# A two-layer diffusion backbone: the MLP output gates as rows from transposes in place of split diagonals, and the last row's sum of three squares on VectorE

## The chip, the cores and the metric

The kernel runs on one core of a Trainium2 chip. The metric is the device time of one execution in microseconds (us), of the whole program from its first to its last instruction. The kernel before takes 1154.96 us, the median of 3 runs (1154.93 to 1155.19). The profile is of one more execution, which took 1155.58 us.

## The reference, cut to what matters

512 latent tokens and 256 context tokens, each a row of 1024 numbers, go through two layers. A layer is a token mixer (pooling in layer 0, attention in layer 1) and an MLP with a squared ReLU and 4096 hidden units. The last layer drops the context.

```python
def rms_norm(x, g):
    return x * lax.rsqrt(jnp.mean(x * x, axis=-1, keepdims=True) + EPS) * g

for i in range(DEPTH):
    sh1, sc1, gt1, sh2, sc2, gt2 = ada_mods(c, w_ada[i], b_ada[i])        # rows of 1024 numbers; ctx has its own
    ...
    x = x + gt1 * rms_norm(y_lat, g_mix_post[i])
    m_lat = jnp.square(jax.nn.relu(modulate(rms_norm(x, g_mlp_pre[i]), sh2, sc2) @ w_mlp_in[i])) @ w_mlp_out[i]
    x = x + gt2 * rms_norm(m_lat, g_mlp_post[i])
```

The change concerns `gt2 * g_mlp_post`, the gate of the MLP's output (for the latent tokens of both layers and for the context tokens of layer 0), and the last `rms_norm`.

## The kernel before, in words

**Tiles and number formats.** Tokens lie in tiles t of 128 rows: 0 to 3 are latent, 4 and 5 context. A product of float32 matrices is three matmuls: each operand is split into a high half (a rounded copy, from ScalarE) and a low half (operand less high half, from VectorE), and high x high, high x low and low x high are added in PSUM. Weights come in pieces of 1 MB by DMA and are split on the way (the halves stand in `units`, L170 and L173). PSUM has two double banks (`psA`) and four single ones (`psB`); three work tiles of 128x1024 in SBUF (`tmp`, called `work`, `diag` or the like) go round.

**The gate.** The conditioning vector's product with `w_ada` ends as columns: entry n of gate k stands in partition n mod 128, column n div 128 (L315, `psada`, gathers the partial sums). The MLP's output has the 1024 channels along a row, so the gate must be turned, and be the same in each of the 128 partitions. The program has two ways. `gate_cols` (L322), in both, multiplies the columns by `g_mlp_post`, one short VectorE operation.
- `gate_diag` (L342 to L356): splits the 8 columns into high and low halves (L346, L347), multiplies the 128x128 identity by them, which gives two tiles `diag` of 128x1024 on VectorE (L350), sums each over the partitions by a matmul of 512 columns against ones (L355: two to a bank, four to a gate), and copies the two banks `psg` to `gate` on ScalarE (L356).
- `gate_rows` (L334) with `gate_half` (L326): transposes each column, broadcast over 128 columns, against the identity, which gives 128x128 of the row per transpose (L332: four to a bank, eight to a gate), and copies the banks to `gate` on ScalarE (L340). The mixers' gates `GT1` are made in this way.

`gate_diag` is called three times: twice in `before0` (L1272), between layer 0's MLP and what follows, for the latent tokens (ci 0) and the context (ci 1), and once in layer 1's last part (L1072), at the step time 5.1.

**The middle.** Layer 0's MLP runs over groups of 256 hidden units. A group is `Seven.run` (L770): seven chains of 12 matmuls, 384 tokens wide (L761, `psin`), into the double banks, with copies on ScalarE (L773 and its like) and two additions on VectorE (L777 and the next), and then `out_mm` (L884): the second product, 6 or 12 matmuls of 512 columns for each half of a row tile, into two banks `pso`, that `out_ev` adds to the sum in `acc` (L898 on VectorE). The last group goes through `finish` (L900) with `last0` (L1231) as its list of steps: for each row tile in turn the mean square (L201 on ScalarE), the power of -1/2 on GpSimd (`rstd`, L214 and L216), the gate (L362), the residual (L365), the next norm, and for each pair of tiles `norm_pair`: transposes (L386, `psx`), scale and shift (L394 on VectorE, the same on ScalarE for other columns), the high half (L400 or L408 on ScalarE) and the low half (L401 or L409 on VectorE), written to `ra`. From those the projections of attention start (L1141, `psq`).

**The end.** In layer 1's last part `finish` goes over the four latent tiles. The last tile's product stands in three banks, 512, 256 and 256 columns wide (`LAST`), and its squares, gates and residual work on these pieces straight from PSUM. `last_rstd` (L1189) adds the first two of the three sums of squares and EPS on GpSimd, the third on ScalarE (L1194), and takes the power on GpSimd (L1195). `norm_g` (L1197) multiplies the three pieces by the gate (L362, kept in program order); the residual (L365) and the store follow.

**The order.** In most places the order on an engine isn't that of the code: the framework's scheduler places instructions by a simulated timeline, and the code's own order (lists of steps with a due time each, `Steps`, L69) sets which comes first where two are ready. `keep_in_program_order` pins an instruction. So a step that is changed at one place can move others at another place.

Of the kernel before, what the change touches and what calls it, by code (L numbers as in the profile page):

```python
# [17 lines left out]
P = 128  # L18
# [76 lines left out]
def backbone(ctx: ExitStack, tc, x, ctx_in, w_ada, w_pool, w_qkv, g_q, g_k, w_o, w_mlp_in,  # L95
# [129 lines left out]
    onesr = const.tile([P, 2], F32R, name="onesr")  # L225
    ve.memset(nhalf, -0.5)
    ve.memset(cond, 0.0)
    ve.tensor_scalar(out=onesr, in0=ident[:, 0:2], scalar1=0.0, scalar2=1.0, op0=ALU.mult, op1=ALU.add)
# [112 lines left out]

    def gate_diag(i, m, ci, to=None):  # L342
        to = ci if to is None else to
        gc = gate_cols(i, m, ci)
        gh = small.tile([P, 2, KT], F32R, tag="gh", name="gh", bufs=2)
        ve.tensor_copy(gh[:, 0, :], gc)  # L346
        ve.tensor_tensor(out=gh[:, 1, :], in0=gc, in1=gh[:, 0, :], op=ALU.subtract)  # L347
        dg = [tmp.tile([P, KT, P], F32R, tag="t", name="diag") for _ in range(2)]
        for z, d in enumerate(dg):
            ve.tensor_tensor(out=d, in0=ident.unsqueeze(1).broadcast_to([P, KT, P]),  # L350
                             in1=gh[:, z, :].unsqueeze(2).broadcast_to([P, KT, P]), op=ALU.mult)
        for h in range(2):
            ps = psB.tile([P, 512], F32, tag="b", name="psg")
            for z, d in enumerate(dg):
                te.matmul(ps, onesr[:, 0:1].broadcast_to([P, P]), d[:, 4 * h:4 * h + 4, :], start=(z == 0), stop=(z == 1))  # L355
            sc.copy(gate[:, to, 512 * h:512 * h + 512], ps)  # L356
# [582 lines left out]
    def mlp1(inner, second, last):  # L939
# [132 lines left out]
        finish(1, [(NG - 2 + q, last_[q].hid, wo_[q]) for q in range(2)], range(NL), last, ((5.1, gate_diag, 1, GT2, 0),))  # L1072
# [108 lines left out]
    def norm_a(t, cols=HALVES):  # L1181
        ss = sm_tile("ss")
        if cols == LAST:
            return last_rstd(t, ss)
        for n, (c0, w) in enumerate(cols):
            mean_square(accv[:, t, c0:c0 + w], ss[:, n:n + 1])
        rs[t] = rstd(ss, len(cols))

    def last_rstd(t, ss):  # L1189
# [4 lines left out]
        sc.activation(ms[:, 1:2], ss[:, 2:3], AF.Identity, scale=1.0, bias=ms[:, 0:1])  # L1194
        gp.tensor_tensor(out=rs[t][:, 0:1], in0=ms[:, 1:2], in1=nhalf[:, 0:1], op=ALU.pow)  # L1195
# [410 lines left out]
```

## Time and profile before

| | |
|---|---|
| median of 3 runs | 1154.96 us |
| the profiled execution | 1155.58 us |
| its span, from the first instruction shown to the last | 1153.7 us |
| TensorE's granted clock, mean | 0.999 of full speed |
| matmul instructions / VectorE / ScalarE / GpSimd | 6200 / 1517 / 1082 / 113 |
| idle time of VectorE in front of L898, waiting for TensorE's L884 | 39.4 us |
| HBM read and written | 138.96 MB and 7.34 MB, 127 GB/s over the span |

How to read the rows shown further down. A row of the timeline has the start (us from the span's start), the time to the end of the last of its instructions, the engine, the line, the operation, its result and operands by the program's names, its shape and type, and the count of like instructions in a row; in brackets the time that the engine stood idle before it, and what ended that. PE is TensorE, PEld its load of weights, DVE VectorE, ACT ScalarE, POOL GpSimd. Matmuls are pipelined: one starts before the one ahead has ended, so the time that a matmul takes from the others is the distance between starts. A row of a table by windows has the stretch, its length, and for TensorE, its weight loads, VectorE, ScalarE and GpSimd the busy time and the count, then the granted clock, the share of the DMA engines and their GB/s. A row of one operation's instances has its durations in ns (shortest, middle, longest) and where the first and the last of them stand.

### The profile page before, as it was taken

What the parts mean: (1) busy time and instruction counts of PE and PEld (TensorE: products, weight loads), DVE (VectorE), ACT (ScalarE), POOL (GpSimd) and SP (SyncE); (2) the same over time, 40 slices, a digit from 0 to 9 for tenths busy, and PEclk for the clock granted to TensorE, in tenths of its full rate; (3) what the DMA queues carried; (4) which work ended last, traced back from release to release, by engine and by line L of the source; (5) the groups of instructions that cost most, each with busy time, mean ns of one, the idle gap of its engine ahead of it and who ended that gap; (6) DMA issues with size and microseconds to landing.
All of it is one profiled execution on the core that took longest, in us unless ns stands there. A gap on an engine that the chain in (4) does not pass through costs nothing.

```text
span 1153.7 us, 16000 instructions
## 1 busy us (share of the span) xinstructions
PE 1135.3 (98%) x6200; PEld 988.7 (86%) x6200; DVE 930.9 (81%) x1517; ACT 632.1 (55%) x1082; POOL 71.1 (6%) x113
## 2 busy tenths in 40 slices
PE   7999999999999999999999999999999999999997
PEld 6779899988899988998887889988988888888886
DVE  4788588998988997996778699867787679778876
ACT  7687445554455444455675367753776435534523
POOL 1230000000000000000241200002100000000001
PEclk9999999999999999999999999999999999999999
DMA  9982233333343444333422102115243214313312
GB/s 376 419 350 75 74 116 113 137 120 141 113 150 140 146 147 146 120 137 115 177 74 73 37 1 74 38 74 186 106 159 133 91 56 146 110 45 138 110 33 114
DMA packets 25516, 147.34 MB, mean 128 GB/s; under 512 B 2784, under 2 KB 5344, under 8 KB 9696
## 3 DMA queue, kind: packets, MB, share of 16 engines
q1 hardware_dynamic: 25440, 146.32, 35.0%
q8 instruction: 49, 0.80, 0.3%
q14 instruction: 27, 0.22, 0.1%
HBM read 138.96 MB, written 7.34 MB: 127 GB/s over the span
## 4 chain that ended last, share of the span: by engine, by line
PE 90%; issue 3%; POOL 3%; DVE 2%; ACT 2%; DMA 0%; POOLq 0%; DVEq 0%; SPq 0%; ACTq 0%
PE pso L884 24%; PE psin L761 18%; PE psin L637 16%; PE pso L995 12%; PE psy L1421 3%; PE po L1396 3%; PE pss L1355 3%; PE psq L1141 2%; PE pspt L1377 2%; PE psin L91 2%; PE psada L91 1%; POOL rs L216 1%; PE psm L91 1%; PE pspool L91 1%; POOL rs L1150 1%
## 5 line engine op out<-in xcount | busy, mean ns | idle before, releaser
L884 PE MATMUL pso<-units,rb 128*128 128x512 f32 x1152 | 279.2, 392 | 0.0
L884 PEld LDWEIGHTS pso<-units,rb 128*128 128x128 f32 x1152 | 214.7, 188 | 41.0
L303 DVE SCALAR_TENSOR_TENSOR rows<-raw,cond,rows 128x256 f32<-128x256 f32 x280 | 127.0, 478 | 2.0
L898 DVE TENSOR_TENSOR acc<-acc,pso 128x512 f32<-128x512 f32 x126 | 83.9, 679 | 39.5 <-PE pso L884 39.4
L637 PE MATMUL psin<-ra,rb 128*128 128x512 f32 (+1 forms) x310 | 87.8, 360 | 0.0
L995 PE MATMUL pso<-units,pairs 128*128 128x512 f32 x336 | 82.7, 389 | 0.0
L637 PE MATMUL psin<-ra 128*128 128x512 f32 (+1 forms) x256 | 76.5, 376 | 0.0
L995 PEld LDWEIGHTS pso<-units,pairs 128*128 128x128 f32 x336 | 63.1, 188 | 13.1
L999 DVE TENSOR_TENSOR acc<-acc,pso 128x512 f32<-128x512 f32 x72 | 48.7, 682 | 26.3 <-PE pso L995 26.3
L214 POOL TENSOR_SCALAR ms<-ss 128x1 f32<-128x1 f32 x15 | 10.0, 666 | 938.2 <-ACT junk L201 917.0
L761 PE MATMUL psin<-ra,units 128*128 128x384 f32 x336 | 65.8, 337 | 0.4 <-ACT psin L773 0.4
L761 PE MATMUL psin<-sums,units 128*128 128x384 f32 x336 | 64.1, 337 | 0.0
L761 PEld LDWEIGHTS psin<-ra,units 128*128 128x128 f32 x336 | 59.9, 188 | 4.0 <-ACT psin L773 0.5
L637 PEld LDWEIGHTS psin<-ra,rb 128*128 128x128 f32 x310 | 55.6, 189 | 8.7
L761 PEld LDWEIGHTS psin<-sums,units 128*128 128x128 f32 x336 | 59.0, 188 | 1.6
L173 DVE TENSOR_TENSOR units<-raw,units 128x1024 fp32r<-128x1024 f32 (+2 forms) x49 | 55.1, 1150 | 6.3 <-ACT units L170 6.1
L170 ACT CAST units<-raw 128x1024 fp32r<-128x1024 f32 (+2 forms) x49 | 47.0, 995 | 17.6 <-PE pso L884 13.4
L637 PE MATMUL psin<-rb 128*128 128x512 f32 (+1 forms) x155 | 55.9, 362 | 0.6 <-DVE rb L1490 0.6
L637 PEld LDWEIGHTS psin<-ra 128*128 128x128 f32 x256 | 47.1, 188 | 8.7
L896 ACT COPY acc<-pso 128x512 f32<-128x512 f32 x48 | 27.1, 586 | 47.3 <-PE pso L884 46.6
L1141 PE MATMUL psq<-units,ra 128*128 128x512 f32 x216 | 52.2, 393 | 0.0
L637 PE MATMUL psin<-rb,ra 128*128 128x512 f32 (+1 forms) x128 | 48.1, 376 | 0.0
(291 smaller groups left out, 2386.5 us busy)
## 6 DMA issues: line engine op xcount, KB each, us to landing
raw<-in_w_ada SPq DMA_DIRECT2D x48, 1024.0 KB, 6.2
raw<-in_w_mlp_in SPq DMA_DIRECT2D x32, 1024.0 KB, 4.9
raw<-in_w_mlp_out SPq DMA_DIRECT2D x32, 1024.0 KB, 5.3
raw<-in_w_qkv SPq DMA_DIRECT2D x6, 1024.0 KB, 4.9
spill<-xr SPq DMA_DIRECT2D x10, 512.0 KB, 3.8
xr<-spill SPq DMA_DIRECT2D x10, 512.0 KB, 6.5
raw<-in_w_o SPq DMA_DIRECT2D x4, 1024.0 KB, 4.9
xr<-in_x SPq DMA_DIRECT2D x4, 512.0 KB, 5.2
```

Source lines behind the costliest of these rows:

```text
L91: return lambda *args, **kw: self.tc.keep_in_program_order(f(*args, **kw))
L170: a = sc.copy(hi, raw)
L173: b = ve.tensor_tensor(out=lo, in0=raw, in1=hi, op=ALU.subtract)
L303: ve.scalar_tensor_tensor(out=r, in0=raw[:, k, :], scalar=cond[:, k, c:c + 1], in1=r, op0=ALU.mult, op1=ALU.add)
L637: te.matmul(ps[:, bank, o:o + ln], w[:, k, fs], rhs, start=start, stop=(k == KT - 1 and n == 2), skip_group_check=len(ks) < KT or self.paired)
L761: te.matmul(bank, w[k], a[k], start=start and k == 0 and m == 0, stop=stop and k == 3 and m == 2, skip_group_check=True)
L884: te.matmul(pss[h][:, 0:cols[h][1]], a[:, f, ts_], w[:, f, cols[h][0]:sum(cols[h])], start=(n == 0 and not seeded[t]), stop=(n == len(seq) ...
L898: ve.tensor_tensor(out=d, in0=d, in1=ps[:, 0:w], op=ALU.add)
L995: te.matmul(ps, a, w, start=(m == 0), stop=(m == len(seq) - 1))
L999: ve.tensor_tensor(out=M[n][:, t], in0=M[n][:, t], in1=ps, op=ALU.add)
L1141: te.matmul(ps, a[:, k, sl], w[:, k % 4, :], start=(k == 0 and n == 0), stop=(k == KT - 1 and n == 2))
L1355: te.matmul(ps[:, c2, 0:384], a[:, sl], b[:, kv, 384 * c2:384 * c2 + 384], start=(n == 0), stop=(n == 2))
```

## The change

1. `gate_diag` goes, with its constant `onesr` and the operation that makes it; its three calls become calls of `gate_rows` at the same places.
2. The last row's sum of the three squares: the third is added on VectorE in place of ScalarE, by an instruction that stands between the second and the third gated piece and is kept there; the power on GpSimd follows it. The scalar operations before (the squares, the first addition on GpSimd) are as before.

```diff
-    onesr = const.tile([P, 2], F32R, name="onesr")
...
-    ve.tensor_scalar(out=onesr, in0=ident[:, 0:2], scalar1=0.0, scalar2=1.0, op0=ALU.mult, op1=ALU.add)
...
-    def gate_diag(i, m, ci, to=None):
-        to = ci if to is None else to
-        gc = gate_cols(i, m, ci)
-        gh = small.tile([P, 2, KT], F32R, tag="gh", name="gh", bufs=2)
-        ve.tensor_copy(gh[:, 0, :], gc)
-        ve.tensor_tensor(out=gh[:, 1, :], in0=gc, in1=gh[:, 0, :], op=ALU.subtract)
-        dg = [tmp.tile([P, KT, P], F32R, tag="t", name="diag") for _ in range(2)]
-        for z, d in enumerate(dg):
-            ve.tensor_tensor(out=d, in0=ident.unsqueeze(1).broadcast_to([P, KT, P]),
-                             in1=gh[:, z, :].unsqueeze(2).broadcast_to([P, KT, P]), op=ALU.mult)
-        for h in range(2):
-            ps = psB.tile([P, 512], F32, tag="b", name="psg")
-            for z, d in enumerate(dg):
-                te.matmul(ps, onesr[:, 0:1].broadcast_to([P, P]), d[:, 4 * h:4 * h + 4, :], start=(z == 0), stop=(z == 1))
-            sc.copy(gate[:, to, 512 * h:512 * h + 512], ps)
...
-        finish(1, [(NG - 2 + q, last_[q].hid, wo_[q]) for q in range(2)], range(NL), last, ((5.1, gate_diag, 1, GT2, 0),))
+        finish(1, [(NG - 2 + q, last_[q].hid, wo_[q]) for q in range(2)], range(NL), last, ((5.1, gate_rows, 1, GT2, 0),))
...
     def norm_a(t, cols=HALVES):
         ss = sm_tile("ss")
         if cols == LAST:
-            return last_rstd(t, ss)
+            final.append(last_rstd(t, ss))
+            return
...
-        sc.activation(ms[:, 1:2], ss[:, 2:3], AF.Identity, scale=1.0, bias=ms[:, 0:1])
-        gp.tensor_tensor(out=rs[t][:, 0:1], in0=ms[:, 1:2], in1=nhalf[:, 0:1], op=ALU.pow)
+        return ss, ms, rs[t]
+
+    def last_pow(ss, ms, r):
+        tc.keep_in_program_order(
+            ve.tensor_scalar(out=ms[:, 1:2], in0=ss[:, 2:3], scalar1=ms[:, 0:1], scalar2=None, op0=ALU.add))
+        gp.tensor_tensor(out=r[:, 0:1], in0=ms[:, 1:2], in1=nhalf[:, 0:1], op=ALU.pow)
...
         for n, (c0, w) in enumerate(cols):
+            if cols == LAST and n == len(cols) - 1:
+                last_pow(*final[0])
             z = gated(t, yg[t], pso[t][n][:, 0:w] if cols == LAST else accv[:, t, c0:c0 + w], c0, c0 + w, pool)
...
-        gate_diag(0, GT2, 0)
-        gate_diag(0, GT2, 1)
+        gate_rows(0, GT2, 0)
+        gate_rows(0, GT2, 1)
```

In the code of the change the functions behind L340 have numbers that are lower by 18, and in `norm_a` and behind it by up to 9: its L743 is L761 of before, L866 is L884, L880 is L898, L344 is L362, L347 is L365, L376 is L394, L383 is L401.

What moves on the engines. **TensorE between the layers**, behind the last small gathering of conditioning sums (`psada`): the last group's chains (`psin`), the gates (`psg`), and its second products (`pso`). Two chains of 12 (L761, with `ra`, `units` and then `rb`, `ra`) stand ahead of the first row here. Before:

```order
L355 MATMUL psg<-diag,onesr 128x512 x2
L761 MATMUL psin<-sums,ra 128x384
L761 MATMUL psin<-rb,ra 128x384
L761 MATMUL psin<-sums,ra 128x384 x2
L761 MATMUL psin<-rb,ra 128x384
L761 MATMUL psin<-sums,ra 128x384 x7
L355 MATMUL psg<-diag,onesr 128x512 x2
L761 MATMUL psin<-ra 128x384 x12
L355 MATMUL psg<-diag,onesr 128x512 x2
L884 MATMUL pso<-units,rb 128x512 x12
L355 MATMUL psg<-diag,onesr 128x512 x2
L884 MATMUL pso<-units,rb 128x512 x84
```

The same place of the change, from `psada` and with those two chains:

```order
L313 MATMUL psada<-parts,sel 32x8 x4
L330 MATMUL psg<-ident,gc 128x128 x16
L743 MATMUL psin<-ra,units 128x384 x12
L743 MATMUL psin<-rb,ra 128x384 x12
L743 MATMUL psin<-sums,ra 128x384
L743 MATMUL psin<-rb,ra 128x384
L743 MATMUL psin<-sums,ra 128x384 x2
L743 MATMUL psin<-rb,ra 128x384
L743 MATMUL psin<-sums,ra 128x384 x7
L743 MATMUL psin<-ra 128x384 x12
L866 MATMUL pso<-units,rb 128x512 x96
```

The four pairs of matmuls, which stood apart between the chains and the second products, have become 16 transposes in a row ahead of the last group's chains, which are alike in both. Further on, between the 16 transposes `psx` of one pair of tiles and the 14 of the next that feed L408, stand 56 other matmuls where there were 72; the 14 that feed L394 at 577.60 us of the profile before have 24 ahead of them since the last two `psx`, where there were 19. The columns of layer 0's gates, of which these transposes are made, stand in VectorE's order some 300 rows ahead of the place that the splits for the diagonals had.

**VectorE a little later**, where the tiles 4 and 5 are scaled and shifted (L394, L376 in the change) and split into low halves (L401, L383). Before:

```order
L394 TENSOR_SCALAR acc<-psx,avec_95,mods_92 128x256 x3
L898 TENSOR_TENSOR acc<-acc,pso 128x512
L394 TENSOR_SCALAR acc<-psx,avec_95,mods_92 128x256 x3
L898 TENSOR_TENSOR acc<-acc,pso 128x512
L362 TENSOR_TENSOR work<-acc,gate 128x512
L401 TENSOR_TENSOR ra<-acc,ra 128x2x256
L173 TENSOR_TENSOR units<-raw,units 128x512
L362 TENSOR_TENSOR work<-acc,gate 128x512
L173 TENSOR_TENSOR units<-raw,units 128x512
L401 TENSOR_TENSOR ra<-acc,ra 128x2x256
```

The same place of the change:

```order
L880 TENSOR_TENSOR acc<-acc,pso 128x512 x2
L344 TENSOR_TENSOR work<-acc,gate 128x512
L376 TENSOR_SCALAR acc<-psx,avec_95,mods_92 128x256 x3
L344 TENSOR_TENSOR work<-acc,gate 128x512
L376 TENSOR_SCALAR acc<-psx,avec_95,mods_92 128x256 x3
L173 TENSOR_TENSOR units<-raw,units 128x512 x2
L347 SCALAR_TENSOR_TENSOR xr<-work,rs,xr 128x1024
L880 TENSOR_TENSOR acc<-acc,pso 128x512
L383 TENSOR_TENSOR ra<-acc,ra 128x2x256
L880 TENSOR_TENSOR acc<-acc,pso 128x512
L173 TENSOR_TENSOR units<-raw,units 128x512 x2
L383 TENSOR_TENSOR ra<-acc,ra 128x2x256
```

Between the last L394 and the first low half stood an addition and a gate before; in the change two halves of a weight, a residual and an addition stand there.

**VectorE's last instructions**, the last tile's gated pieces and residuals. Before:

```order
L365 SCALAR_TENSOR_TENSOR xr<-work,rs,xr 128x512 x2
L362 TENSOR_TENSOR work<-pso,gate 128x512
L362 TENSOR_TENSOR work<-pso,gate 128x256 x2
L365 SCALAR_TENSOR_TENSOR xr<-work,rs,xr 128x640
L365 SCALAR_TENSOR_TENSOR xr<-work,rs,xr 128x384
```

The same place of the change:

```order
L347 SCALAR_TENSOR_TENSOR xr<-work,rs,xr 128x512 x2
L344 TENSOR_TENSOR work<-pso,gate 128x512
L344 TENSOR_TENSOR work<-pso,gate 128x256
L1183 TENSOR_SCALAR ms<-ss,ms 128x1
L344 TENSOR_TENSOR work<-pso,gate 128x256
L347 SCALAR_TENSOR_TENSOR xr<-work,rs,xr 128x640
L347 SCALAR_TENSOR_TENSOR xr<-work,rs,xr 128x384
```

The sum (L1183) has come between the second and the third piece. In layer 0's MLP, from 290 to 492 us of the profile before, and up to the end of the projections for keys and values, near 620 us, TensorE, VectorE and ScalarE have the same instructions in another order; ahead of it and from there on to layer 1's last part, the rows are alike but for the numbers of buffers. GpSimd's rows are alike everywhere. On SP's queue the second of the three last loads of projection weights (L151) stands ahead of three of the four loads of the rotary tables (L1120), behind which it stood before.

More of the change, by code (lines that the diff above doesn't have):

```diff
@@ L1187, in norm_a @@
         rs[t] = rstd(ss, len(cols))
+    final = []
     def last_rstd(t, ss):
@@ L1470, in attention @@
         at(45.691, lambda: split(*raws[3], q=3))
-        at(39.281, gate_diag if False else gate_rows, 1, GT1, 0)
+        at(39.281, gate_rows, 1, GT1, 0)
     def output(st, base):
```

## The prediction

> **What bounds the kernel now.** I read the page first (the span, the busy shares, the chain that ended last), then the timeline of the three places that the change touches.
>
> ```profile
> span 1153.7 us, 16000 instructions
> PE 1135.3 (98%) x6200; PEld 988.7 (86%) x6200; DVE 930.9 (81%) x1517; ACT 632.1 (55%) x1082; POOL 71.1 (6%) x113
> PE 90%; issue 3%; POOL 3%; DVE 2%; ACT 2%; DMA 0%; POOLq 0%; DVEq 0%; SPq 0%; ACTq 0%
> ```
>
> TensorE holds 90% of the chain, so an edit pays only where it takes TensorE time away, ends one of the few waits of TensorE, or shortens the end after its last matmul. VectorE is busy 81% of the span, yet work taken from it is worth nothing by itself: the six diagonals and their splits are VectorE time beside a running TensorE. What a matmul costs is the distance of starts, not the duration, since matmuls overlap.
>
> **Place 1, the last gate (1126 to 1131 us).**
>
> ```profile
> 1129.90 1.09 PE L355 MATMUL psg<-diag,onesr 128*128 128x512 f32 x4
> 1130.82 1.52 PE L884 MATMUL pso<-ra,units 128*128 128x512 f32 x6
> 1132.18 1.52 PE L884 MATMUL pso<-units 128*128 128x512 f32 x6
> ```
>
> Six 512-wide matmuls take 1132.18 - 1130.82 = 1.36 us, 0.227 each. The four diagonal matmuls take 1130.82 - 1129.90 = 0.92. TensorE shows no idle time here, so this is on the path. Eight transposes replace them, and transposes of the same kind (fp32, 128 columns, against the identity) stand in the trace:
>
> ```profile
> 577.60 1.69 PE L386 MATMUL psx<-ident,acc 128*128 128x128 f32 x14
> 579.05 6.83 PE L884 MATMUL pso<-units,rb 128*128 128x512 f32 x29
> 585.72 1.91 PE L386 MATMUL psx<-ident,acc 128*128 128x128 f32 x16
> ```
>
> From 577.60 to 585.72 are 8.12 us; 29 matmuls take 29 x 0.227 = 6.58, so 14 transposes cost 1.54, or 0.11 each. Eight cost 0.88: **-0.04 us**. On VectorE the gate's columns alone are left, without the splits and diagonals behind them, so the transposes are not late.
>
> **Place 2, the two gates between the layers (536 to 554 us).**
>
> ```profile
> 540.43 2.35 PE L761 MATMUL psin<-ra,units 128*128 128x384 f32 x12 [0.43 <-ACT psin L773]
> 544.71 0.62 PE L355 MATMUL psg<-diag,onesr 128*128 128x512 f32 x2
> 546.05 1.39 PE L761 MATMUL psin<-sums,ra 128*128 128x384 f32 x7
> 547.47 0.73 PE L355 MATMUL psg<-diag,onesr 128*128 128x512 f32 x2
> 547.47 0.56 DVE L777 TENSOR_TENSOR work<-work,psin 128x384 f32<-128x384 f32 x1
> 548.08 2.36 PE L761 MATMUL psin<-ra 128*128 128x384 f32 x12
> 550.28 0.62 PE L355 MATMUL psg<-diag,onesr 128*128 128x512 f32 x2
> 550.74 2.89 PE L884 MATMUL pso<-units,rb 128*128 128x512 f32 x12
> 553.47 0.62 PE L355 MATMUL psg<-diag,onesr 128*128 128x512 f32 x2
> 553.93 6.33 PE L884 MATMUL pso<-units,rb 128*128 128x512 f32 x27
> ```
>
> Three of the four pairs of diagonal matmuls cost TensorE time: 550.74 - 550.28 = 0.46, 553.93 - 553.47 = 0.46, and as much the one at 544.71, together 1.38 us. The fourth, at 547.47, costs nothing: the chain before it ends at 546.05 + 1.39 = 547.44, L777 must read that bank before the next chain may write it (547.47 + 0.56 = 548.03), and the next chain starts at 548.08. That wait stays when the pair goes, and no other work stands in it. So of four pairs one is no gain.
>
> The 16 transposes now stand together, between the small psada matmuls and the chain at 540.43. They cost 16 x 0.11 = 1.76 us and fill the 0.43 us in which TensorE waits for L773: 1.33 more. A matmul starts before the one ahead ends (the pair at 550.28 takes 0.62 and is passed after 0.46), so they can begin 0.16 earlier: 1.17. The place gives 1.17 - 1.38 = **-0.2 us** (0 at the other end). Their inputs, the gate's columns, stand some 300 rows ahead in VectorE's order. Of the four ScalarE copies of the gates two stood beside the chains; now all four do, ahead of a relu that waits for L777 anyway.
>
> **Place 3, what is reordered (290 to 492 and 554 to 620 us).** The scheduler places the same instructions otherwise.
>
> ```profile
> 290.00:492.00 202.00, 202.00 (x1023) 181.82 (x1022) 179.10 (x340) 96.14 (x144) 0.00 (x0) 1.00 0.40 141
> ```
>
> In the first stretch TensorE is busy all 202 us, and two independent streams (the next group's psin, this group's pso) lie before it: I take 0, with +0.6 us as the far end (a wait as long as the longest below) and nothing to win. In the second, the kernel before has two waits that may go:
>
> ```profile
> 611.78 0.30 PEld L1141 LDWEIGHTS psq<-rb,ra 128*128 128x128 f32 x2 [0.34 <-ACT ra L408]
> 613.09 2.14 PEld L1141 LDWEIGHTS psq<-rb,ra 128*128 128x128 f32 x10 [0.59 <-DVE ra L409]
> ```
>
> They are 0.93 us. In the order of the change, 56 matmuls in place of 72 stand between the two groups of transposes there, so those that feed L408 come 16 x 0.227 = 3.6 us earlier; VectorE's table work keeps its place among what it waits for. On the other side the first low half for the projections comes later: VectorE does two weight halves (L173) and a residual (L365) ahead of it, where before they stood behind:
>
> ```profile
> 579.40 1.45 DVE L394 TENSOR_SCALAR acc<-psx,avec,mods 128x256 f32<-128x256 f32 x3 [0.55 <-PE psx L386]
> 583.92 0.69 DVE L401 TENSOR_TENSOR ra<-acc,ra 128x512 fp32r<-128x512 f32 x1
> 587.38 4.81 PE L1141 MATMUL psq<-rb,ra 128*128 128x512 f32 x20
> 589.34 1.28 DVE L173 TENSOR_TENSOR units<-raw,units 128x512 fp32r<-128x512 f32 x2
> 591.45 1.27 DVE L365 SCALAR_TENSOR_TENSOR xr<-work,rs,xr 128x1024 f32<-128x1024 f32 x1
> ```
>
> Before, the low half begins 583.92 - 579.40 = 4.5 us after the first L394, and 3.5 us ahead of its projections. The added 1.28 + 1.27 us take it to 586.5, and the L394 themselves come 0.8 later (in the order 24 matmuls in place of 19 stand ahead of their transposes: 5 x 0.227 = 1.1, less the 0.2 above): 587.3. TensorE starts six matmuls on high halves at about 587.2, so it asks for the low half at 588.5: 1.2 us to spare if nothing waits. On SP's queue a weight load now stands ahead of three of the four loads of the rotary tables:
>
> ```profile
> 590.64 27.90 SPq L151 DMA_DIRECT2D raw<-in_w_qkv  x2
> 605.59 0.69 DVE L1126 TENSOR_TENSOR acc<-acc,grow 128x512 f32<-128x512 f32 x1
> ```
>
> It goes out at 590.64, when the last L173 has freed its buffer; the tables are first touched at 605.59, 15 us later, so their loads cost nothing. For the stretch I take **-0.1 us**, between +1.1 and -0.93.
>
> **Place 4, the end.**
>
> ```profile
> 1148.09 0.42 DVE L362 TENSOR_TENSOR work<-pso,gate 128x256 f32<-128x256 f32 x1 [0.94 <-ACT junk L201]
> 1148.53 0.56 POOL L1195 TENSOR_TENSOR rs<-ms,nhalf 128x1 f32<-128x1 f32 x1 [1.54 <-ACT ms L1194]
> 1149.12 1.42 DVE L365 SCALAR_TENSOR_TENSOR xr<-work,rs,xr 128x640 f32<-128x640 f32 x2 [0.61 <-POOL rs L1195]
> ```
>
> L1194 goes; the same sum stands on VectorE ahead of the third gated piece. Its like is at the program's start:
>
> ```profile
> 6.01 0.15 DVE L91 TENSOR_SCALAR ms<-ss 128x1 f32<-128x1 f32 x1 [4.25 <-ACT junk L91]
> 6.25 0.56 POOL L492 TENSOR_TENSOR rs<-ms,nhalf 128x1 f32<-128x1 f32 x1 [4.96 <-DVE ms L91]
> 6.84 0.75 DVE L91 TENSOR_SCALAR acc<-xr,rs 128x1024 f32<-128x1024 f32 x1 [0.68 <-POOL rs L492]
> ```
>
> The power starts 0.24 after the sum's start, and the operation that uses it 0.59 after that. The third gated piece waited for the last square (its bracket), which the sum needs too, so the sum starts at 1148.09, the power at 1148.33 and the residual at 1148.92 in place of 1149.12: **-0.20 us**. Queued behind the sum is that piece; its 0.42 us lie under the power, to about 1148.66. If it held the power back until then, the residual would start at 1148.66 + 0.59 = 1149.25, +0.13 us. Rows of both kinds:
>
> ```profile
> 587.67 1.31 POOL L214 TENSOR_SCALAR ms<-ss 128x1 f32<-128x1 f32 x1 [6.61 <-DVE acc L898]
> 588.74 0.68 DVE L898 TENSOR_TENSOR acc<-acc,pso 128x512 f32<-128x512 f32 x1
> 589.07 0.56 POOL L216 TENSOR_TENSOR rs<-ms,nhalf 128x1 f32<-128x1 f32 x1
> 591.68 2.06 POOL L216 TENSOR_TENSOR rs<-ms,nhalf 128x1 f32<-128x1 f32 x1
> ```
>
> The power at 589.07 took 0.56 beside an L898, which reads one operand from PSUM as the gated piece does; the one at 591.68 took 2.06 beside L365, with both from SBUF. I take no hold. The Trainium skill (SBUF — State Buffer, section "SBUF: two separate sides") says that VectorE with two SBUF inputs locks a port pair that GpSimd's reads share; by it the gated piece, with one PSUM input, doesn't hold the power: the two rows agree.
>
> **Sum.** -0.04 - 0.2 - 0.1 - 0.20 = -0.54 us. The profiled execution took 1155.58 us, 1.88 more than its span, so its like would take 1155.04. It is 0.62 above the median of the runs, 1154.96; the difference carries over: **1154.4 us**. What a measurement of this kernel can tell from no change is about 0.2%, 2.3 us, so the forecast is within it.
>
> **Rivals.**
> 1. Slower: TensorE waits for the low halves at about 588 us. The L365 that now stands ahead of them waits for a sum and a power on GpSimd that come while L173 runs, with both its inputs in SBUF. Held ones took 1.31 and 2.06 us above, 3.4 together, where a free power takes 0.56 and a free sum less: some 2.4 longer. 1.2 us of it is to spare, so it costs 2.4 - 1.2 = 1.2, and the total is -0.44 + 1.2 = +0.8: 1155.7 us. It decides from 1.2 us of hold on, and turns the sign at 1.65. For it: those rows are of this very stretch. Against: before, the same holds were absorbed.
> 2. The two waits at 611 to 613 go and nothing new comes: -0.44 - 0.93 = -1.4, 1153.6 us. Against: L408 is reached through VectorE, which has no less to do.
> 3. Transposes don't overlap.
>
> ```profile
> L332 PE MATMUL psg<-ident,gc x8: 271/272/273, 764.9 to 766.7; 128*128 128x128 f32 x8
> ```
>
> At 0.272 each, Place 2 gives 16 x 0.272 - 0.43 - 1.38 = +2.54 and Place 1 8 x 0.272 - 0.92 = +1.26; with the end, +3.6: 1158.6 us. The 14 at 577.60 speak against it. The Trainium skill (TensorE: Matmul & The Clock Gate, "Part 4: PE-mode transpose") gives about 275 ns for a 128x128 transpose within a kernel: that is the duration here, and the 0.11 us between starts differ from it, so the measurement decides.
> 4. The stretch from 290 to 492 us gets waits of its own, one to four of 0.6 us: -0.54 + 0.6 to + 2.4, 1155.0 to 1156.8 us.
>
> That the change doesn't do what it says is excluded by the order: the sum stands between the second and third piece, and no diagonal is left.
>
> **Chances.** Forecast (1153.9 to 1155.0) 0.5; rival 1 0.25; rival 2 0.15; rival 3 0.03; rival 4 0.07. The range for eight in ten reaches over rivals 1 and 2 with the bounds of the reordered stretches: 1153.0 to 1156.4 us. Faster by over 0.2% needs rival 2 and more, 0.08; slower by over 0.2% is rival 3 and the far ends of 1 and 4, 0.10; within, 0.82.
>
> **What would show it.** The profile after should have 16 transposes right behind psada near 540 us, still a wait of TensorE for L777 near 548, the chain into the last layer 0.2 us earlier; no wait for low halves near 588 (else rival 1), less than 0.9 us of waits near 612; eight transposes of 0.88 us near 1130; and a power of 0.56 us that starts 0.24 after the sum, with the residual 0.83 after the sum's start. A held power, a TensorE wait in the two reordered stretches, or a distance of transposes over 0.11 us would make the forecast wrong.

## The result: 1.2% slower, and the profile after

The changed kernel takes 1169.66 us (median of 4 runs, 1169.21 to 1169.82), the kernel before 1155.08 us in the same session (1154.93 to 1155.79): a ratio of 1.0122, 95% interval 1.011 to 1.0135. The profiled execution took 1169.82 us and has a span of 1168.0 us, 14.3 longer than the 1153.7 of before. The forecast was 1154.4 us, with 1153.0 to 1156.4 as its range. One execution of e5 below, at a mean granted clock of 0.856, took 2158 us and is left out of e5's numbers.

The page of the changed kernel, the lines that answer to the first three of before:

```profile
span 1168.0 us, 16013 instructions
PE 1147.2 (98%) x6212; PEld 989.8 (85%) x6212; DVE 924.9 (79%) x1505; ACT 632.7 (54%) x1081; POOL 69.4 (6%) x113
PE 48%; issue 45%; POOL 3%; ACT 2%; DVE 1%; DMA 0%; POOLq 0%; DVEq 0%; SPq 0%; ACTq 0%
```

TensorE has 12 matmuls more and is busy 11.9 us longer (1147.2 against 1135.3). Twelve matmuls more, 24 small transposes where 12 wide ones were, can't take that: the same matmuls have become slower. VectorE lost 6 us of work, as the edit meant, and that bought nothing. (The chain that ended last now shares TensorE's stretches between PE and "issue"; the sum, 93%, is what it was.)

The groups of TensorE's instructions say which matmuls. Columns: line, operation, operands, shape, count, then busy us and mean ns of one. Before:

```profile
L884 PE MATMUL pso<-units,rb 128*128 128x512 f32 x1152 | 279.2, 392 | 0.0
L995 PE MATMUL pso<-units,pairs 128*128 128x512 f32 x336 | 82.7, 389 | 0.0
L1141 PE MATMUL psq<-units,ra 128*128 128x512 f32 x216 | 52.2, 393 | 0.0
L995 PE MATMUL pso<-ra,pairs 128*128 128x512 f32 x168 | 39.4, 389 | 0.0
```

After:

```profile
L866 PE MATMUL pso<-units,rb 128*128 128x512 f32 x1152 | 283.6, 395 | 0.0
L977 PE MATMUL pso<-units,pairs 128*128 128x512 f32 x336 | 85.0, 396 | 0.0
L1123 PE MATMUL psq<-units,ra 128*128 128x512 f32 x216 | 53.6, 398 | 0.0
L977 PE MATMUL pso<-ra,pairs 128*128 128x512 f32 x168 | 39.4, 389 | 0.0
```

Every 512-wide group with an operand in `units` is dearer: 2.3 us over 336 matmuls is 6.8 ns each, 4.4 us over 1152 is 3.8. The group shown without `units` isn't. Nothing in the diff touches these matmuls.

Three rows of TensorE's timeline show the second loss, at the place that the forecast called Place 3:

```profile
590.56 1.94 PE L368 MATMUL psx<-ident,acc 128*128 128x128 f32 x16
592.88 1.19 PE L1123 MATMUL psq<-rb,ra 128*128 128x512 f32 x4 [0.39 <-ACT ra L382]
596.41 6.05 PE L1123 MATMUL psq<-rb,ra 128*128 128x512 f32 x18 [2.34 <-ACT ra L382]
```

Before, the 20 projections here ran without a gap. Now TensorE waits for ScalarE's high halves (L382), 2.34 us at one time.

Place 1 and the end, from two more views of the timeline after:

```profile
1144.07 1.03 PE L330 MATMUL psg<-ident,gc 128*128 128x128 f32 x8
1144.86 1.65 PE L866 MATMUL pso<-ra,units 128*128 128x512 f32 x6
```

```profile
1161.97 0.39 ACT L201 ACTIVATE junk<-pso 128x256 bf16<-128x256 f32 x1 [0.94 <-PE pso L866]
...
1162.55 0.21 DVE L1183 TENSOR_SCALAR ms<-ss,ms 128x1 f32<-128x1 f32 x1 [1.03 <-ACT junk L201]
1162.68 0.41 DVE L344 TENSOR_TENSOR work<-pso,gate 128x256 f32<-128x256 f32 x1
1162.85 0.56 POOL L1184 TENSOR_TENSOR rs<-ms,nhalf 128x1 f32<-128x1 f32 x1 [1.42 <-DVE ms L1183]
1163.44 1.41 DVE L347 SCALAR_TENSOR_TENSOR xr<-work,rs,xr 128x640 f32<-128x640 f32 x2 [0.35 <-POOL rs L1184]
```

Eight transposes take 0.79 us there, and the end does what was forecast, a little less of it. Both places gain.

### The profile page after: what moved, and what is told of

The parts are those of the page before. It is cut to its first block, busy times and chain, and to the rows that moved or that the text cites. A ratio compares the mean times of both kernels' runs of the same rounds, so it can differ in the third digit from the quotient of the medians.

```text
span 1168.0 us, 16013 instructions
## 1 busy us (share of the span) xinstructions
PE 1147.2 (98%) x6212; PEld 989.8 (85%) x6212; DVE 924.9 (79%) x1505; ACT 632.7 (54%) x1081; POOL 69.4 (6%) x113
## 4 chain that ended last, share of the span: by engine, by line
PE 48%; issue 45%; POOL 3%; ACT 2%; DVE 1%; DMA 0%; POOLq 0%; DVEq 0%; SPq 0%; ACTq 0%
PE psin L619 15%; PE pso L977 12%; PE psq L1123 4%; PE psy L1412 3%; PE po L1387 3%; PE pss L1346 3%; PE pso L866 2%; PE pspt L1368 2%; POOL rs L216 1%; PE psada L91 1%; PE psm L91 1%; PE pspool L91 1%; POOL ms L208 1%; POOL rs L1132 0%; POOL ms L214 0%
## 5 line engine op out<-in xcount | busy, mean ns | idle before, releaser
L866 PE MATMUL pso<-units,rb 128*128 128x512 f32 x1152 | 283.6, 395 | 0.0
L866 PEld LDWEIGHTS pso<-units,rb 128*128 128x128 f32 x1152 | 214.8, 188 | 44.7
L880 DVE TENSOR_TENSOR acc<-acc,pso 128x512 f32<-128x512 f32 x126 | 83.5, 679 | 43.4 <-PE pso L866 43.3
L743 PE MATMUL psin<-ra,units 128*128 128x384 f32 x336 | 65.7, 338 | 0.0
L743 PE MATMUL psin<-sums,units 128*128 128x384 f32 x336 | 63.8, 338 | 0.0
L743 PEld LDWEIGHTS psin<-ra,units 128*128 128x128 f32 x336 | 59.7, 188 | 3.8 <-ACT psin L755 0.3
L743 PEld LDWEIGHTS psin<-sums,units 128*128 128x128 f32 x336 | 59.0, 188 | 1.8
```

The source lines that it names most:

```text
L743: te.matmul(bank, w[k], a[k], start=start and k == 0 and m == 0, stop=stop and k == 3 and m == 2, skip_group_check=True)
L866: te.matmul(pss[h][:, 0:cols[h][1]], a[:, f, ts_], w[:, f, cols[h][0]:sum(cols[h])], start=(n == 0 and not seeded[t]), stop=(n == len(seq) ...
L880: ve.tensor_tensor(out=d, in0=d, in1=ps[:, 0:w], op=ALU.add)
```

## The experiments

**Theory A: addresses.** With `onesr` (8 bytes, 32 with rounding) and the two buffers of `gh` (64 each) gone, `units`, which is allocated behind them, starts 160 bytes earlier in each partition: at 124672 in place of 124832, as the built program places it. Two readings: A1, what counts is how the starts of a matmul's two operands stand to each other; A2, where one of them starts. The rival is that the new order alone costs all of it.

**e1_room**: the change with unused tiles in the places of the two that went. All tiles start where they did before, and the order is that of the change, row for row.

```diff
+    const.tile([P, 2], F32R, name="room")
+    for _ in range(2):
+        small.tile([P, 2, KT], F32R, tag="gh", name="room", bufs=2)
```

> The change with two unused tiles in place of the removed ones (8 bytes for onesr, 2 x 64 bytes for gh, in each partition), so that every tile stands at its address of the kernel before; the order of instructions is that of the change, row for row. Theory A (addresses: without those tiles units and all that lies behind it stand 160 bytes lower, so its rows start at 0 in place of 32 modulo 64 bytes, and the 512-wide matmuls that read it need 0.233 us in place of 0.227): the distance goes back to 0.227 and 10 us go; what is left over before are the waits of TensorE at 592 to 600 us, some 4.2 us: 1159.3 us. Theory B (order: matmuls are slower because other work stands beside them, and the addresses don't matter): 1169.7 us as the change.

Measured: 1160.25 us, ratio 1.0039 [1.0025, 1.0052], span 1158.6. Room that nobody uses gives 9.4 us of the 14.3 back (1168.0 - 1158.6). The other 4.9 stay, so neither theory has all of it.

**e2_plus32, e3_minus32**: the change with the first of the two unused tiles only (`units` 32 bytes up from the change); and the kernel before with `onesr` put into the slot of `nhalf` (`units` 32 bytes down from before, the order of before).

```diff
+    const.tile([P, 2], F32R, name="room")
```

```diff
-    nhalf = const.tile([P, 4], F32, name="nhalf")
+    nhalf = const.tile([P, 8], F32, name="nhalf")
...
-    onesr = const.tile([P, 2], F32R, name="onesr")
-    ve.memset(nhalf, -0.5)
+    onesr = nhalf[:, 4:6].bitcast(F32R)
+    ve.memset(nhalf[:, 0:4], -0.5)
```

> The change with one unused tile of 8 bytes (32 with the rounding), so units starts at 32 modulo 64 bytes again, but 128 bytes lower than in the kernel before. Theory A, if only the place modulo 64 bytes counts: 1159.3 us, as with all the room given back. Theory A, if the place modulo 128 or 256 bytes counts: something between that and 1169.7 us. Theory B: 1169.7 us.

> The kernel before, with onesr put into the free bytes behind nhalf, so that its own slot of 32 bytes goes: units starts at 0 modulo 64 bytes, the diagonals and the order between the layers are those of before (the order differs in some ten rows). Theory A: 2,900 matmuls of 512 columns at up to 0.0066 us more each, some 10 us, 1165 us. Theory B: 1155.1 us.

Measured: e2 1169.01 us, 1.0117 [1.0104, 1.0131]; e3 1164.41 us, 1.0074 [1.0059, 1.009]. 32 bytes are no remedy, and e3 makes the kernel before 9 us slower (span 1162.7) with no gate changed.

**e6_rarb, e7_all32, e8_minus256**: which places matter. e6 is the kernel before with `nhalf` allocated behind `rb`, so that `ra` and `rb` start 32 bytes lower and `units` does not; e7 has e3's edit as well, so that all three go down together and `pairs` alone stays; e8 is the change with fewer small buffers, which puts `units` a further 96 bytes down, 256 from its place before.

```diff
-    nhalf = const.tile([P, 4], F32, name="nhalf")
     grow = const.tile([P, 2, HD], F32, name="grow")
...
     rb = const.tile([P, 10240], F32R, name="rb")
+    nhalf = const.tile([P, 4], F32, name="nhalf")
```

```diff
-        return small.tile([P, 8], F32, tag=tag, name=tag, bufs=2 if tag == "gc" else 8)
+        return small.tile([P, 8], F32, tag=tag, name=tag, bufs={"gc": 2, "sm": 5}.get(tag, 8))
```

> The kernel before with nhalf allocated behind rb: ra and rb stand 32 bytes lower, units and all else where they were; the order of instructions is that of before, row for row. Theory A1 (what counts is that the moving and the stationary operand start at the same place modulo some hundred bytes): slow, at 0.233 us, become the 512-wide matmuls of units with rb or ra, and of ra or rb with pairs; those of units with pairs, and of ra and rb among themselves, stay at 0.227; about 1163 us. Theory A2 (what counts is where the moving operand alone starts): all that move ra or rb become slow, all that move units stay; about 1163 us too. The groups tell them apart, not the time.

> The kernel before with nhalf behind rb and onesr within nhalf's slot: ra, rb and units stand all three 32 bytes lower, the tiles on the other side (pairs among them) where they were. Theory A1: only the matmuls with pairs become slow, some 590 by 0.0066 us, 3.9 us: 1159.5 us. Theory A2: all 3,000 become slow: 1170 us or more.

> The change with five buffers in place of eight for one small tile that is hardly used, so that units stands 256 bytes lower than in the kernel before (the change itself: 160 lower); the order is that of the change, row for row. If the starts count modulo 256 bytes or less: 0.227 us, and the time of e1, 1160 us. If they count modulo 512 or more: 0.232 us or so, 1169 us.

Measured: e6 1164.11 us, 1.0077 [1.0063, 1.0091]; e7 1159.44, 1.0033 [1.002, 1.0046]; e8 1160.83, 1.0044 [1.003, 1.0057], the time of e1. Groups of e6:

```profile
L884 PE MATMUL pso<-units,rb 128*128 128x512 f32 x1152 | 283.2, 395 | 0.0
L995 PE MATMUL pso<-units,pairs 128*128 128x512 f32 x336 | 83.6, 392 | 0.0
...
L995 PE MATMUL pso<-ra,pairs 128*128 128x512 f32 x168 | 40.5, 395 | 0.0
```

And of e7:

```profile
L884 PE MATMUL pso<-units,rb 128*128 128x512 f32 x1152 | 278.5, 391 | 0.0
L995 PE MATMUL pso<-units,pairs 128*128 128x512 f32 x336 | 84.7, 395 | 0.0
...
L995 PE MATMUL pso<-ra,pairs 128*128 128x512 f32 x168 | 40.5, 395 | 0.0
```

Between these two only `units` moved. `units,rb` became fast, `units,pairs` slow: the same start of `units` is good with one partner and bad with the other, which A2 can't give. All runs on this, with the starts modulo 256 bytes (from the built programs) and the mean ns of each group:

| run | ra | rb | units | pairs | units,rb | units,pairs | units,ra | ra,pairs | rb,pairs |
|---|---|---|---|---|---|---|---|---|---|
| before, e1, e8 | 160 | 160 | 160 | 160 | 392 | 389 | 393 | 389 | 389 |
| change | 160 | 160 | 0 | 160 | 395 | 396 | 398 | 389 | 391 |
| e2 | 160 | 160 | 32 | 160 | 395 | 394 | 397 | 389 | 391 |
| e3 | 160 | 160 | 128 | 160 | 395 | 396 | 398 | 389 | 390 |
| e6 | 128 | 128 | 160 | 160 | 395 | 392 | 398 | 395 | 396 |
| e7 | 128 | 128 | 128 | 160 | 391 | 395 | 393 | 395 | 395 |

A pair of operands is fast where its two columns agree and slow where they differ (distances of 32, 128 and 160 bytes were tried; 160 is 96 counted the other way round). The exceptions are small: `rb,pairs` in the change, e2 and e3, `units,pairs` in e6, and the 42 matmuls with both operands in `units` (389 ns before, 393 in the change) agree and take 1 to 4 ns more; in the program they stand between slow ones. e8's `units` lies 256 bytes lower and is fast, so the period is 256 bytes or a divisor of it; e2's, at a distance of 128, is slow with each partner, so it isn't 128 or a divisor of that. A1 is shown, with a period of 256 bytes. What in the chip makes it so is not.

**Theory B: the new order.** What is left of the loss, 4.9 us, is in e1's span. First, which edit:

**e10_mid**: before, with only the two gates between the layers changed. **e4_tail**: before, with only layer 1's gate and the last sum changed. Both keep the addresses.

```diff
-        gate_diag(0, GT2, 0)
-        gate_diag(0, GT2, 1)
+        gate_rows(0, GT2, 0)
+        gate_rows(0, GT2, 1)
```

```diff
-        finish(1, [(NG - 2 + q, last_[q].hid, wo_[q]) for q in range(2)], range(NL), last, ((5.1, gate_diag, 1, GT2, 0),))
+        finish(1, [(NG - 2 + q, last_[q].hid, wo_[q]) for q in range(2)], range(NL), last, ((5.1, gate_rows, 1, GT2, 0),))
...
-        sc.activation(ms[:, 1:2], ss[:, 2:3], AF.Identity, scale=1.0, bias=ms[:, 0:1])
...
+            ve.tensor_scalar(out=ms[:, 1:2], in0=ss[:, 2:3], scalar1=ms[:, 0:1], scalar2=None, op0=ALU.add))
```

> The kernel before with the two edits at the end alone (the last gate from eight transposes, the last sum on VectorE between the second and the third gated piece); the tiles keep their addresses, since the diagonals of layer 0 stay. By the prediction's terms -0.04 and -0.20: 1154.8 us. If the tail were part of the loss (a held power, transposes that are dear): 1155.3 us or more.

> The kernel before with the two gates between the layers from transposes, and nothing else; layer 1's gate keeps its diagonals, so the tiles keep their addresses. The order between the layers is that of e1, row for row. If the new order there is the whole of what e1 leaves: 1160.0 us, with the waits of TensorE at 586 to 596 us. If the edits at the end have a part in it: nearer to 1155.7 us.

Measured: e4 1155.83 us, 1.0 [0.9991, 1.0009]; e10 1160.71 us, 1.0049 [1.0033, 1.0064], span 1159.0. The gates between the layers hold all of the 4.9 us. e1's timeline near 588 us (behind L340 its line numbers are 15 lower than those of before: L379 is L394, L385 is L400, L350 is L365, and so on):

```profile
580.40 1.28 DVE L350 SCALAR_TENSOR_TENSOR xr<-work,rs,xr 128x1024 f32<-128x1024 f32 x1 [3.74 <-POOL rs L216]
581.60 1.28 DVE L883 TENSOR_TENSOR acc<-acc,pso 128x512 f32<-128x512 f32 x2
...
583.40 1.44 DVE L379 TENSOR_SCALAR acc<-psx,avec,mods 128x256 f32<-128x256 f32 x3
...
586.95 1.94 PE L371 MATMUL psx<-ident,acc 128*128 128x128 f32 x16 [0.90 <-DVE acc L379]
...
588.59 1.66 ACT L385 CAST ra<-acc 128x512 fp32r<-128x512 f32 x3
589.26 1.20 PE L1126 MATMUL psq<-rb,ra 128*128 128x512 f32 x4 [0.38 <-ACT ra L385]
...
592.12 0.62 ACT L385 CAST ra<-acc 128x512 fp32r<-128x512 f32 x1
...
592.80 5.77 PE L1126 MATMUL psq<-rb,ra 128*128 128x512 f32 x18 [2.34 <-ACT ra L385]
```

The residual and the last of these high halves before:

```profile
577.57 1.28 DVE L365 SCALAR_TENSOR_TENSOR xr<-work,rs,xr 128x1024 f32<-128x1024 f32 x1 [2.09 <-POOL rs L216]
...
589.95 0.63 ACT L400 CAST ra<-acc 128x512 fp32r<-128x512 f32 x1
```

The first scaling of tiles 4 and 5 starts at 583.40; before it was 579.40. Ahead of it stand a residual that waited 3.74 us for GpSimd (2.09 before), two additions and a gate. What follows is late by 2 to 4 us, through VectorE's freeing of the banks `psx` (0.90) to ScalarE's high halves (0.38 and 2.34). And the pause has a price behind it. By windows (length; busy and count of TensorE, its weight loads, VectorE, ScalarE, GpSimd; granted clock; DMA share; GB/s), e1:

```profile
589.03:592.44 3.41, 1.20 (x4) 0.67 (x4) 3.41 (x6) 3.41 (x9) 0.00 (x0) 1.00 0.06 19
592.44:595.85 3.41, 3.05 (x7) 2.48 (x8) 3.41 (x7) 3.38 (x8) 2.07 (x3) 0.50 0.76 245
595.85:599.27 3.42, 3.42 (x16) 2.82 (x16) 3.42 (x6) 1.98 (x4) 1.45 (x2) 1.00 1.04 329
```

For 3.41 us, most of them after the pause, the granted clock is 0.50, and seven matmuls start in the time of thirteen. By starts of matmuls the place loses 1.06, 0.56, 2.51, 0.37 and 1.16 us (the last is six matmuls at up to 0.427 in place of 0.227), 5.66 in all; the two waits of before at 611 to 613, 0.81, are gone: +4.85.

Why the residual is late: theory C puts it down to the first tile of the last second products, whose sum VectorE adds at 560.01 in e1 and at 558.03 before; rival D to the order at the pair of tiles alone, the additions and the gate that now stand ahead of the scaling.

**e5_pin4, e9_pin45**: e1 with the first tile brought forward. The second products of tile 4 (in e9 of 4 and 5, with tile 4's in six groups) are kept in program order.

```diff
-            te.matmul(pss[h][:, 0:cols[h][1]], ...
+            z = te.matmul(pss[h][:, 0:cols[h][1]], ...
+            if i == 0 and len(parts) > 1 and t in (4,):
+                tc.keep_in_program_order(z)
```

```diff
+            if i == 0 and t == 4:
+                order.sort(key=lambda z: ((z[0] >= 6) + (z[0] >= 9), z[1]))
...
-            if i == 0 and len(parts) > 1 and t in (4,):
+            if i == 0 and len(parts) > 1 and t in (4, 5):
```

> The kernel of e1_room, with the 24 matmuls of the last group's second product for row tile 4 (the first in the list of finish) kept in program order; nothing else is asked for, and the scheduler then places the second tile's matmuls behind them, and the projections as in the kernel before. Theory C (the 4.6 us that e1 leaves come from the first tile: its 24 matmuls stand interleaved by sixes with those of the second tile, so its sum is complete 2.0 us later, and its chain of norm, residual, transposes and high halves with it): TensorE's waits at 586 to 596 us go, 1155.0 us. Rival D (VectorE's and ScalarE's own order, or operations held on GpSimd, make the high halves late whatever the first tile does): 1158 to 1160 us.

> As e5_pin4, but the 24 matmuls of row tile 4 in another order: six of each half that need nothing of the last group, then three of each that need its first 128 hidden units, then the last three of each (e5 put nine of the first half ahead of the second half, and TensorE waited 2.2 and 0.4 us for the hidden units). The first tile is then complete some 2 us earlier than in e1, and nothing waits for the hidden units. Theory C: no wait at 551 to 556 and none at 586 to 596 us, 1155.5 us (the waits at 602 and 615 us of e5, 1.2 and 1.3 us, may stay: 1157 us at most). Rival D: 1158 to 1160 us, with new waits for the high or low halves.

Measured: e5 1160.91 us, 1.0046 [1.0032, 1.006]; e9 1158.61 us, 1.0031 [1.0019, 1.0043]. The first sum came at 558.66 and 557.21, and the waits near 588 went. But others came: TensorE now waited for the hidden units' halves at 552 to 555 (2.3 us in e5, 1.0 in e9), for a norm of ScalarE at 601 to 604 (1.06 and 1.10), and again at 613 to 617.

**e11_late_gate, e12_gate5**: e1 with the latent tokens' gate made later, among the steps of the last group.

```diff
     def last0(st, n, t):
+        if n == 0:
+            st.at(15.5, gate_rows, 0, GT2, 0)
...
-        gate_rows(0, GT2, 0)
```

e12 has 5.25 in place of 15.5.

> The kernel of e1_room (every tile at its address of before), with the latent tokens' gate of layer 0 made later: its call of gate_rows stands as a step of the last group's list (time 15.5) in place of before0, and no matmul is pinned. Two copies of psg in place of four then stand on ScalarE ahead of the relus of the last group's hidden units, as in the kernel before, and the second tile's matmuls are no longer all ahead of the first tile's last ones. Theory C2 (the four copies, 2.06 us in a row, make the hidden units 0.85 us later, the first tile's sum 2.0 us later, and so its high halves): no wait of TensorE over 0.3 us between 585 and 597 us, 1155.0 us within 0.5. Rival D (the halves are late through VectorE's and GpSimd's order in any case, once the diagonals are gone): 1158 to 1160 us.

> As e11_late_gate, with the step of the latent tokens' gate at 5.25 in place of 15.5: its eight transposes stand behind the second tile's matmuls, and the first transposes of the pair of tiles 4 and 5 behind all 96 matmuls of four tiles, as in the kernel before, in place of behind 72 (there TensorE waited 1.75 us for them). Theory C2: neither that wait nor those at 585 to 597 us: 1155.5 us, the kernel before within 0.5 us. Rival D: 1157 to 1160 us.

Measured: e11 1157.51 us, 1.0019 [1.0009, 1.0028]; e12 1157.26, 1.0015 [1.0006, 1.0024], span 1155.5. In e12 three of the 4.9 us come back (1158.6 - 1155.5); e11 waits 1.57 us for its first transposes of the pair, near 570. But e12's first sum stands at 559.68, as late as in e1, and so does the residual:

```profile
580.08 1.28 DVE L350 SCALAR_TENSOR_TENSOR xr<-work,rs,xr 128x1024 f32<-128x1024 f32 x1 [3.15 <-POOL rs L216]
581.28 1.44 DVE L379 TENSOR_SCALAR acc<-psx,avec,mods 128x256 f32<-128x256 f32 x3
...
588.31 4.81 PE L1126 MATMUL psq<-rb,ra 128*128 128x512 f32 x20
```

Here the scaling stands right behind the residual, and the 20 projections run without a gap. So a late first tile by itself doesn't cost the wait: theory C falls as the sole cause. (What e12 still loses are waits of 0.15 to 0.65, near 551, 556, 601, 613 and 615.)

**e13_pair_later**: the kernel before, with the pair's due time later, so that the additions and gates stand ahead of the scaling while the first tile keeps its time. With this edit the load of the rotary tables comes ahead and writes over the place of tiles 4 and 5 in `acc`, so that the context's keys and values are made from the tables; the instructions are the same.

```diff
-            st.at([18.2, 28.6, 39][n // 2], norm_pair, t - 1, 1, 0, hH, hL, True, (True, True, False)[n // 2],
+            st.at([20.9, 28.6, 39][n // 2], norm_pair, t - 1, 1, 0, hH, hL, True, (True, True, False)[n // 2],
```

> The kernel before, diagonals and all, with one due time changed: the step norm_pair of tiles 4 and 5 at 20.9 in place of 18.2. Ahead of 575 us the order is that of before; behind it VectorE does two additions and two gates ahead of the first scaling of the pair (L394) and a residual ahead of the second, and ScalarE's order is nearly that of the change. Theory E (the waits of TensorE at 586 to 596 us come from VectorE's and ScalarE's order at the pair alone, whatever the gates and the first tile do): waits there that add up to 3 us or more, with matmuls at half speed behind them, 1159 to 1161 us. Theory C (they come from the gates or the first tile ahead of it): 1155.6 us, within 0.5.

Measured: 1156.97 us, 1.0013 [1.0004, 1.0023], span 1155.2.

```profile
577.91 1.28 DVE L365 SCALAR_TENSOR_TENSOR xr<-work,rs,xr 128x1024 f32<-128x1024 f32 x1 [2.09 <-POOL rs L216]
...
582.35 1.44 DVE L394 TENSOR_SCALAR acc<-psx,avec,mods 128x256 f32<-128x256 f32 x3
...
589.78 0.62 ACT L400 CAST ra<-acc 128x512 fp32r<-128x512 f32 x1
...
590.46 3.76 PE L1141 MATMUL psq<-rb,ra 128*128 128x512 f32 x14 [1.57 <-ACT ra L400]
```

The residual is on time; the order alone gives one wait of 1.57 us for the high halves, and the clock after it stays at 1.00:

```profile
590.46:593.40 2.94, 2.93 (x12) 2.12 (x13) 2.94 (x7) 2.43 (x6) 2.03 (x3) 1.00 0.92 332
```

So the four cases stand as a square: neither (before), no wait at 585 to 597; the late residual alone (e12), none; the order alone (e13), one that costs 1.7 us by starts; both (e1, e10), 5.66. By TensorE's starts at 573 and 620 us, which count all that is lost or won between them, e12 loses 0.96, e13 1.2 and e1 4.84 us, so the two together cost 2.7 more than their sum. Neither C nor D is enough; the loss needs both, and the half clock, 1.16, is part of it. The square is not quite clean: e12 and e13 have orders of their own at other places. No kernel tried here beats the one before.

Why the first tile is late is read from rows and was not tried by itself. Before:

```profile
548.00 1.07 ACT L356 COPY gate<-psg 128x512 f32<-128x512 f32 x2 [2.98 <-PE psg L355]
...
548.96 0.86 ACT L784 ACTIVATE work<-work 128x768 f32<-128x768 f32 x1
```

In e1:

```profile
548.58 2.06 ACT L341 COPY gate<-psg 128x512 f32<-128x512 f32 x4 [1.96 <-PE psin L746]
...
550.49 0.88 ACT L769 ACTIVATE work<-work 128x768 f32<-128x768 f32 x1
```

Four copies instead of two stand on ScalarE ahead of the relu (L769, L784 before), which comes 1.5 us later, and the scheduler then mixes the second products of tiles 4 and 5. The four copies are not the only way there: in e12 two stand ahead of the relu, which starts at 551.66 all the same, since twelve matmuls of the second products have moved ahead of the last group's chains.

## Why the prediction was wrong, by its own steps

**Addresses: a term that wasn't there, +9.4 us.** The forecast costed the removal of `onesr` and `gh` at nothing, without saying so. It listed what instructions the edit removes, adds and moves; two small tiles that go also move each tile behind them. This is the largest error, and no sum over instructions would have found it. The Trainium skill (SBUF — State Buffer, section "SBUF: two separate sides") says that on the engines' side only the port pair shared by VectorE and GpSimd causes contention, and that TensorE never waits. That section names no cost for how the starts of a matmul's two operands stand to each other; the 4 to 7 ns measured for each 512-wide matmul whose operands start apart are such a cost.

**Place 3, forecast -0.1, measured +4.85: the step that failed.** The range there was +1.1 to -0.93. The forecast had it that "the L394 themselves come 0.8 later", from TensorE's transposes alone (5 x 0.227 less 0.2 is 0.9; the transposes came 1.3 later, at 578.90 against 577.60). They came 4.0 later (583.40 against 579.40), since VectorE does two additions and a gate ahead of them, rows that the order in the part on the change shows, and a residual that waited 1.65 us longer. The forecast counted what stood ahead of the low halves, not what stood ahead of the scaling on which low and high halves both rest. It then asked when TensorE needs the low halves; what it waited for were ScalarE's high halves. Rival 1 had the sign and the place, a wait near 588 us behind a held residual, but that was luck in part: it went by low halves, its residual is the next one, which waited only 0.46 us (588.46 in e1), and it gave the wait 1.2 us. It had no clock that drops: 1.16 us.

**Place 2, forecast -0.2, measured -0.2: right in its time, wrong in one reason.** In e1, whose matmuls have the old speed:

```profile
540.13 0.25 PE L316 MATMUL psada<-parts,sel 128*32 128x8 f32 x8
540.31 1.96 PE L333 MATMUL psg<-ident,gc 128*128 128x128 f32 x16
542.02 2.36 PE L746 MATMUL psin<-ra,units 128*128 128x384 f32 x12
...
573.19 0.38 PE L371 MATMUL psx<-ident,acc 128*128 128x128 f32 x2
```

Before:

```profile
539.75 0.25 PE L315 MATMUL psada<-parts,sel 128*32 128x8 f32 x8
...
573.02 0.38 PE L386 MATMUL psx<-ident,acc 128*128 128x128 f32 x2
```

From `psada` to `psx` are 33.06 us against 33.27, -0.21; the 16 transposes take 542.02 - 540.31 = 1.71 (1.76 forecast), and rival 3 with its 0.272 each is out. The wrong reason: the four copies, "ahead of a relu that waits for L777 anyway". The relu waited for the copies too, 0.42 us more than before (550.49 is 1.91 after L762's start; 548.96 was 1.49 after L777's), and so Place 3 began late.

**290 to 492 us**, forecast 0 with +0.6 as the far end: from the first second product to `psada` e1 takes 0.26 us more. Rival 4 names the kind; its waits of 0.6 us and more didn't come.

**Place 1, forecast -0.04**: 0.79 in place of 0.92, -0.13. **Place 4, forecast -0.20**: the power starts 0.30 after the sum, takes 0.56 and isn't held; the residual starts 1.47 us after the start of the last square (1163.44 - 1161.97), before 1.57, so -0.10: half, since the sum started 0.04 later behind the square than the gated piece had, and the power 0.30 after it in place of 0.24. The rotary loads behind a weight load cost nothing that the trace shows, as forecast.

The sum: 9.4 + 4.85 + 0.26 - 0.21 - 0.13 - 0.10 = 14.1 us; the spans differ by 14.3, and 0.2 have no place here.

## What to carry to other kernels

A tile that is taken out moves all that is allocated behind it: compare the operands' starts modulo 256 bytes before and after, and keep the room if they change; one run with the old addresses and the new order splits the two effects at once. Where a schedule moves, count everything that now stands ahead of the first operation of a chain, on each engine that feeds the waiting one, not only what stands ahead of its last. A change that takes work from an engine that isn't the bound gains nothing by itself, and what it pulls together (four copies in a row, by the rows of e1) can make another engine late.

## What the hardware showed that was not expected

A 512-wide fp32r matmul has starts 0.227 us apart when its two operands start at the same place modulo 256 bytes, and some 4 to 7 ns more when they don't: 2 to 3% of such a matmul, 0.8% of this kernel. What stays open: distances other than 32, 128 and 160 bytes; why the second product of layer 0 (`units,rb`) takes 392 ns, 3 above the best, although its starts agree.

In the five traces with the long pause (the change, e1, e2, e8, e10) the granted clock was 0.50 for one stretch of 3.41 us. In every trace the stretches at one clock, but for the last, are whole multiples of 3.41 us long (170 or 171 of them up to this one), as if the clock were set anew with a fixed beat. In the beat ahead of the low one TensorE was busy 1.07 to 1.36 of the 3.41 us. In e5 it stood 2.06 us in one go, across the border of two beats:

```profile
550.01:553.43 3.42, 2.28 (x12) 1.67 (x10) 0.71 (x1) 3.39 (x5) 0.00 (x0) 1.00 1.00 408
553.43:556.84 3.41, 2.23 (x8) 1.53 (x9) 1.21 (x2) 0.84 (x2) 0.00 (x0) 1.00 1.02 412
```

There the clock stayed at 1.00, and so it did behind beats with 1.84 us of work in e11 and 2.08 in e13 (pauses of 1.57 each). So either a pause between 2.06 and 2.34 us is the limit, or work between 1.36 and 1.84 us in a beat; no run tells the two apart. One of e1's four executions took 1159.05 us, 1.1 less than the next, at a mean clock of 0.999 where the others had 0.997 or 0.998: that would be the same pause without the half clock, but of it there is no trace. The Trainium skill (TensorE: Matmul & The Clock Gate, "Part 1: The HAM clock gate") gives an idle window of about 3.4 us for the step to half speed. The length agrees with the beat here; but the beat was not idle, and the measurement decides.
